# One encoder layer on one core: S5's transfers on another queue, weights asked for earlier, and smaller edits around them

## The chip, the core and the metric

The kernel runs on one core of a Trainium2 chip. The core has five engines with a queue of instructions each: TensorE (PE, matrix products into PSUM), VectorE (DVE), ScalarE (ACT), GpSimd (POOL) and SyncE (SP, which here issues DMAs only). DMAs can be issued from SP, ACT or POOL. An engine takes its instructions in the order of its queue; an instruction whose inputs aren't there holds up all behind it. The metric is the device time of one execution in microseconds (us); the profile's span runs from the first to the last instruction.

## What is computed

One layer of an encoder on 512 tokens of width 1024, all in float32. Cut to what matters:

```python
h = rms_norm(x, attn_norm_g)
a_q, a_ckv, a_iq, a_ik, a_iw, s5_u, c_qkv, c_z, c_a, c_b, gates = split(h @ w_in)
y_a = dsa_attention(a_q, a_ckv, a_iq, a_ik, a_iw, ...) @ w_proj_a   # top-128 keys of an indexer, then softmax
y_b = s5_branch(s5_u, ...) @ w_proj_b                               # complex diagonal recurrence, gelu, gated unit
y_c = gdn_branch(c_qkv, c_z, c_a, c_b, ...) @ w_proj_c              # gated delta rule in chunks of 64
g_a, g_b, g_c = split(sigmoid(gates))
x = x + (g_a * y_a + g_b * y_b + g_c * y_c) @ w_out
x = x + conv_glu_ffn(rms_norm(x, ffn_norm_g), w_up, ffn_conv_w, w_down)
return rms_norm(x, final_norm_g)
```

In `s5_branch` the last step is the gated unit, `y * sigmoid(y @ w_glu)`. In `gdn_branch` a triangular system of 64 rows is solved for each chunk and head; the kernel forms the inverse instead.

## The kernel before

**Products.** float32 accuracy comes from three fast products for each: `split` writes an operand as a high part (`wh`, an ACT cast) and a low part (`wl`, a DVE subtraction), and `dense` sums high x high, high x low and low x high. `wload` (L272) fetches a 128x1024 weight tile `w` by DMA from SP's queue and splits it; there are two buffers of `w` and two pairs `wh`, `wl` in the first half of the kernel. A third pair, `self.wx`, is foreseen but stays `None`. `proj(i)` (L326) loads tile i of `w_in` and runs the 24 matmuls of 128x512 into one of two PSUM buffers `ps_acc`; its caller empties the buffer. With GP = 3, behind the S5 stage every third load's low part is computed on POOL (L285) instead of DVE (L256).

**Stages up to the feed-forward part.** (1) Start: x and the first four weight tiles arrive, the tiles of `s5_u` are projected, the norm is formed (`rB`), `u` is stored to DRAM (`ud`, L1405) and the normed input is split into `hh`, `hl`. (2) S5: `s5_uu` (L570) reads U back from `ud`, for each half of the groups twice, into the lower and the upper 64 partitions; `s5_setup` and `s5_half` form tables; `s5_state` runs two scans a call, `s5_out` forms y and stores it to `yd` (L708); `s5_main` reads it back as `yT` (L602), splits it, multiplies by `w_glu`, and for each of four tiles computes tanh on ACT (L623), `(tanh + 1) * yT` on DVE (L624) and a permuted copy times 0.25 on ACT (`s_bo`, L628), which goes to DRAM (`obd`). Woven into it are the projections for 18 gates (`gates`, whose tanh is stored to DRAM from SP's queue, L1260) and rounds of the indexer's top-k (`topk`: MAX8 and MATCH_REPLACE on DVE). (3) The delta rule: 12 projections with a convolution on DVE (`gdn_in`, L753 to L758), then `gdn_main`, with attention's projections, the rest of the gates and the top-k woven in; `gdn_main` inverts the chunks' triangles: 16-row blocks on DVE (L902 to L927), then 32-row and 64-row blocks by small products on PE (L940 to L977), which are woven with attention and with `merge` of branch b. (4) The merges, `w_out`, the feed-forward part and the last norm.

**Order.** The Python code weaves these parts by hand (the strings `ORD`, `OR1`, `OR2`, `OR3` and the rates `R_...` say which generator gives the next step). The order of the code isn't yet that of the queues: the kernel is built with `schedule_with_timeline_sim=True`, and a planner simulates the engines by its own model of durations and fills each queue with what it holds ready, earlier code first. `issue_after` binds an instruction behind another on its engine. On the chip the queues run as planned, whatever the true durations are.

Of the kernel before, what the change touches and what calls it, by code (L numbers as in the profile page):

```python
# [157 lines left out]
GP = 3  # L158
KV = 'acc'
OR3 = 'ttgztgzttggtttttggzggttt'  # L160
XO = 'w0,t0,w0,t1,w1,t2,t3,x0,x1,x2,x3,w2'
# [12 lines left out]
NBIG = 5  # L174
R_QKV = 0.606
# [49 lines left out]
class _K:  # L225
# [46 lines left out]
    def wload(self, src, n=1024, hl=None):  # L272
# [4 lines left out]
        if hl is None:  # L277
            if self.wx and self.wi % 3 == 0:
                hl = [self.wx.tile([128, 1024], F32R, tag="x" + z, name="w" + z, bufs=1) for z in "hl"]
            else:  # L280
                hl = [self.wp.tile([128, 1024], F32R, tag="w" + z, name="w" + z, bufs=self.wb) for z in "hl"]
# [43 lines left out]

    def proj(self, i):  # L326
        wh, wl = self.wload(self.I["w_in"][i])
        ps = self.acc()
        self.dense(ps, wh, wl, self.hh, self.hl, 8)
        return ps  # L330
# [39 lines left out]
    def s5_setup(self):  # L370
# [27 lines left out]
        tt(t0, dt, P("are"), OP.mult)  # L398
        with self.tc.issue_after(self.lastp.ins):
            exact_exp(mag, t0)  # L400
# [168 lines left out]
    def s5_uu(self):  # L569
# [3 lines left out]
        v = self.ud.rearrange("(h b m) (j c) -> h (m j) b c", h=2, m=16, j=4)  # L573
        for hf in range(2):
            U = self.s5.tile([128, 16, 128], F32, tag="U", name="s5_U", bufs=2)
            for r in range(2):
                nc.sync.dma_start(U[r * 64:r * 64 + 64], v[hf])
# [3 lines left out]
    def s5_main(self):  # L581
        nc = self.nc
        self.yd = self.dp.tile([512, 512], F32, tag="yd", name="s5_yd", bufs=1)
        self.yyh, self.yyl = [], []
        self.s5q = []
# [14 lines left out]
        for n in range(4):  # L600
            t = self.s5.tile([128, 512], F32, tag="b2", name="s5_yT", bufs=self.nb2)
            nc.sync.dma_start(t, self.yd[n * 128:(n + 1) * 128])  # L602
# [9 lines left out]
        for n2 in range(2):  # L612
            wh, wl = glu[n2]
            for j in range(2):
# [9 lines left out]
                nc.vector.scalar_tensor_tensor(s, s, 1.0, yT[n], OP.add, OP.mult)  # L624
                sv = s.rearrange("p (t c) -> p t c", t=4)
                pv = lambda x: x.rearrange("p (c t) -> p t c", t=4)
                bo = self.s5.tile([128, 512], F32, tag="b2", name="s5_bo", bufs=self.nb2)
                nc.scalar.activation(pv(bo), sv, AF.Identity, scale=0.25)  # L628
                nc.sync.dma_start(obd[:, n], bo)
# [3 lines left out]
    def s5_state(self, hf, o, WT, CA, T, cosT, sinT, m4):  # L633
# [33 lines left out]
        sr = q.tile([128, 4, 129], F32, tag="sr", name="s5_sr", bufs=2)  # L667
        si = q.tile([128, 4, 129], F32, tag="si", name="s5_si", bufs=2)
        nc.gpsimd.memset(sr[:, :, 0:1], 0.0)
        nc.gpsimd.memset(si[:, :, 0:1], 0.0)  # L670
# [10 lines left out]
    def s5_out(self, hf, o, WT, CA, T, S):  # L681
# [17 lines left out]
        for g in range(2):  # L699
# [7 lines left out]
            for a2 in range(2):  # L707
                nc.sync.dma_start(yv[hf][g][a2], yy[rows[a2]].rearrange("p (b c) -> p b c", b=4))  # L708
# [66 lines left out]
    def gdn_main(self):  # L775
# [167 lines left out]
        for h0 in (0, 2):  # L943
# [8 lines left out]
            for h in range(2):  # L952
                pc = ps[:, h * 256:h * 256 + 256].rearrange("p (t a b) -> p t a b", b=32, t=4)
                tt(half(P1[h], 0).rearrange("p (t a) b -> p t a b", t=4), pc, _bc(half(self.C("m32"), 0), 1, 4), OP.mult)
            for h in range(2):
                pxy = self.acc("sm")
                for t in range(4):
                    c = slice(t * 128, (t + 1) * 128)
                    self.mm(pxy[0:64, 256 + t * 32:256 + t * 32 + 32], YF[0:64, h0 + h, t * 128:t * 128 + 64],
                            P1[h][0:64, t * 128:t * 128 + 32])  # L960
                    self.mm(pxy[:, t * 64:t * 64 + 64], P1[h][:, c], half(YF[:, h0 + h, c], 1))
# [5 lines left out]
        for h in range(4):  # L967
            ps = self.acc("sm")
            N4, X4, Y4, P4 = v4(NT[:, h]), v4(XF[:, h]), v4(YF[:, h]), v4(P1h())
            for t in range(4):  # L970
                self.mm(ps[64:128, t * 64:t * 64 + 64], N4[0:64, t, 64:128], X4[0:64, t, 0:64])
            nc.scalar.copy(P4[64:128, :, 0:64], ps[64:128, 0:256].rearrange("p (t c) -> p t c", t=4))
            py = self.acc("sm")
            for t in range(4):
                self.mm(py[0:64, t * 64:t * 64 + 64], P4[64:128, t, 0:64], Y4[64:128, t, 64:128])
            nc.scalar.copy(Y4[0:64, :, 64:128], py[0:64, 0:256].rearrange("p (t c) -> p t c", t=4))
            yield 1  # L977
# [146 lines left out]
    def attn(self):  # L1124
# [14 lines left out]

        def keys(j):  # L1140
# [6 lines left out]
            kl = [ap.tile([128, 512], F32R, tag="kl%d" % z, name="a_kl", bufs=2) for z in range(2)]  # L1147
# [470 lines left out]
```

## Time and profile before

| | us |
|---|---|
| median of 3 runs (lowest to highest) | 956.65 (956.61 to 957.61) |
| the profiled execution, its own time | 957.42 |
| its span | 955.7 |
| PE busy | 918.5 (96%) |
| DVE busy | 645.3 (68%) |
| ACT busy | 419.5 (44%) |
| POOL busy | 84.4 (9%) |

The profile is one execution. "Busy" of PE means that a matmul is under way; matmuls overlap, so what PE could do faster doesn't show in that number. A full matmul of 128x512 starts every 0.23 us at the clock of 2.4 GHz and every 0.43 us at 1.2 GHz; which of the two is granted stands in the column of the clock. The rows on which the prediction rests stand below, under the diff.

### The profile page before, as it was taken

To read this page: it belongs to the slowest core of one execution; us is meant where nothing else is said; L and a number is where in the kernel's file an instruction comes from. 1 tells how busy PE (TensorE), PEld (TensorE's weight loads), DVE (VectorE), ACT (ScalarE), POOL (GpSimd) and SP (SyncE) were. 2 spreads that over 40 slices of the span, in tenths; PEclk is the share of its full clock that TensorE was granted. 3 is DMA by queue.
4 is the path that set the end of the run, shared out by engine and by line. 5 is a ranking of instruction groups with operands and counts; after the bars stand their busy time and mean duration, and the time that the engine had idled before them with its cause. 6 is when DMAs were issued, how large, how long until landed. Compare 5 with 4: busy or idle time off the path is not lost. (4 is left out here: it accounts for less than half of the span.)

```text
span 955.7 us, 12705 instructions
## 1 busy us (share of the span) xinstructions
PE 918.5 (96%) x4780; PEld 746.2 (78%) x4780; DVE 645.3 (68%) x1119; ACT 419.5 (44%) x761; POOL 84.4 (9%) x93
## 2 busy tenths in 40 slices
PE   7989999896999999899999999999999999999997
PEld 5768877675888777778868888988888888888885
DVE  5969497988998779546677736667666676622423
ACT  6574443235565653237852314443444434322212
POOL 3001000110123411311011000000000000000000
PEclk9999999997999999989999999999999999999999
DMA  8585334441224645523108723232323223223212
GB/s 319 152 192 147 108 99 132 144 134 65 88 89 121 171 122 165 155 89 121 34 12 278 229 100 109 94 107 90 109 89 102 96 88 110 89 95 104 88 67 88
DMA packets 55917, 114.54 MB, mean 120 GB/s; under 512 B 15664, under 2 KB 22192, under 8 KB 55856
## 3 DMA queue, kind: packets, MB, share of 16 engines
q1 hardware_dynamic: 53776, 110.33, 36.4%
q0 software_dynamic: 2080, 3.41, 1.8%
q8 instruction: 37, 0.61, 0.3%
q14 instruction: 24, 0.20, 0.1%
HBM read 95.89 MB, written 14.42 MB: 115 GB/s over the span
## 5 line engine op out<-in xcount | busy, mean ns | idle before, releaser
L256 DVE TENSOR_TENSOR wl<-w,wh 128x1024 fp32r<-128x1024 f32 (+1 forms) x127 | 153.0, 1206 | 146.2 <-ACT wh L255 145.8
L255 ACT CAST wh<-w 128x1024 fp32r<-128x1024 f32 (+1 forms) x127 | 131.7, 1037 | 192.3 <-PE ps_acc L247 80.7
L247 PE MATMUL ps_acc<-hh,wh 128*128 128x512 f32 x376 | 152.6, 406 | 12.7 <-ACT g_raw L753 10.1
L247 PE MATMUL ps_acc<-hh,wl 128*128 128x512 f32 x376 | 151.6, 403 | 1.3 <-DVE wl L256 1.3
L247 PE MATMUL ps_acc<-hl,wh 128*128 128x512 f32 x376 | 149.5, 398 | 0.0
L247 PEld LDWEIGHTS ps_acc<-hh,wh 128*128 128x128 f32 x376 | 72.1, 192 | 28.7 <-ACT g_raw L753 10.5
L247 PEld LDWEIGHTS ps_acc<-hh,wl 128*128 128x128 f32 x376 | 72.0, 192 | 19.3 <-DVE wl L256 2.6
L247 PEld LDWEIGHTS ps_acc<-hl,wh 128*128 128x128 f32 x376 | 72.1, 192 | 15.4 <-issue 0.5
L247 PE MATMUL ps_acc<-f_hh,wh 128*128 128x512 f32 x160 | 62.3, 389 | 0.0
L247 PE MATMUL ps_acc<-f_hl,wh 128*128 128x512 f32 x160 | 62.3, 389 | 0.0
L247 PE MATMUL ps_acc<-f_hh,wl 128*128 128x512 f32 x160 | 62.2, 389 | 0.0
L247 PE MATMUL ps_sm<-f_hh,wh 128*128 128x512 f32 x160 | 62.2, 389 | 0.0
L247 PE MATMUL ps_sm<-f_hl,wh 128*128 128x512 f32 x160 | 62.2, 389 | 0.0
L247 PE MATMUL ps_sm<-f_hh,wl 128*128 128x512 f32 x160 | 62.2, 389 | 0.0
L285 POOL TENSOR_TENSOR wl<-w,wh 128x1024 fp32r<-128x1024 f32 x13 | 34.9, 2687 | 186.2 <-ACT wh L284 171.1
L255 ACT CAST ah<-f_th 128x512 fp32r<-128x512 f32 x22 | 13.7, 621 | 58.1 <-DVE f_th L1554 58.1
L247 PEld LDWEIGHTS ps_acc<-f_hl,wh 128*128 128x128 f32 x160 | 30.0, 188 | 6.3
L247 PEld LDWEIGHTS ps_sm<-f_hh,wh 128*128 128x128 f32 x160 | 30.1, 188 | 6.2
L247 PEld LDWEIGHTS ps_acc<-f_hh,wl 128*128 128x128 f32 x160 | 30.1, 188 | 6.2
L247 PEld LDWEIGHTS ps_sm<-f_hl,wh 128*128 128x128 f32 x160 | 30.0, 188 | 6.2
L247 PEld LDWEIGHTS ps_sm<-f_hh,wl 128*128 128x128 f32 x160 | 30.0, 187 | 6.2
L247 PEld LDWEIGHTS ps_acc<-f_hh,wh 128*128 128x128 f32 x160 | 30.0, 187 | 6.1
(532 smaller groups left out, 1984.4 us busy)
## 6 DMA issues: line engine op xcount, KB each, us to landing
w<-in_w_in_dram SPq DMA_DIRECT2D x50, 512.0 KB, 3.6
w<-in_w_up_dram SPq DMA_DIRECT2D x44, 512.0 KB, 3.3
w<-in_w_down_dram SPq DMA_DIRECT2D x22, 512.0 KB, 3.3
gd<-m_th SPq DMA_DIRECT2D x24, 256.0 KB, 2.2
m_th<-gd SPq DMA_DIRECT2D x24, 256.0 KB, 3.7
w<-in_w_out_dram SPq DMA_DIRECT2D x8, 512.0 KB, 4.3
sq<-in_x_dram SPq DMA_DIRECT2D x4, 512.0 KB, 8.9
s_U<-s_ud SPq DMA_DIRECT2D x4, 512.0 KB, 8.9
```

What stands on the lines that cost most here:

```text
L247: return self.nc.tensor.matmul(out, lhsT, rhs, start=start, stop=stop)
L255: self.lasta = nc.scalar.copy(hi, src)
L256: self.lastv = nc.vector.tensor_sub(lo, src, hi.bitcast(F32))
L285: nc.gpsimd.tensor_tensor(l[:, :n], w[:, :n], h[:, :n].bitcast(F32), OP.subtract)
```

## The change

- S5's transfers go to POOL's queue: the store of `u` of the start, the reads of U, the store and the read back of `yd`, the store of `obd`. U is read in quarters into the lower 64 partitions, and the upper 64 are copied from the lower ones within SBUF.
- The gated unit: DVE writes the permuted `bo` itself; ACT's copy is gone, and the factor 0.25 is applied in `fetch`, by the split.
- Inverse products: in the 32-row step all products of one shape come first and then those of the other, for two heads at once; in the 64-row step two heads share a PSUM tile and a copy.
- Weights: `proj` takes its pair from a list that `ahead` fills: after the matmuls of a projection, the loads of the next two (in S5 three) are put into the code, in the order `PLAN`. In S5 the pair `wx` exists, for every third load of the first 20.
- GP = 0: no weight split on POOL.
- Stores of gates go from ACT's queue. The states' tiles `sr`, `si` are four fixed ones, whose first column is cleared once. The zero halves of the keys `kl` are written for the first two of four only.
- At the start: `rB` is cleared and 12 products of 128x128 on it run first; w2 is asked for before the rows of x; `t0` and `mag` of S5's setup wait for the split of the fourth weight tile.

```diff
@@ -155,10 +155,10 @@
...
-GP = 3
+GP = 0
...
-XO = 'w0,t0,w0,t1,w1,t2,t3,x0,x1,x2,x3,w2'
+XO = 'w0,t0,w0,t1,w1,t2,t3,w2,x0,x1,x2,x3'
@@ -172,6 +172,9 @@
...
+PLAN = [27, 28, 29, 30, 31, 21, 22, 32, 33, 34, 35, 36, 37, 38, 39, 40, 41, 42, 43, 44, 8, 9, 10, 11, 4, 5, 6, 7, 12, 13, 14, 15,
+        20, 16, 17, 18, 19, 45, 46, 23, 47, 24, 48, 49, 50, 25, 26]
+N_WX = 20
@@ -269,13 +272,13 @@
...
-    def wload(self, src, n=1024, hl=None):
+    def wload(self, src, n=1024, hl=None, extra=False):
...
-            if self.wx and self.wi % 3 == 0:
+            if self.wx and extra and self.fpos % 3 == 0:
@@ -323,10 +326,23 @@
...
+    def ahead(self, n):
...
+        while len(self.fq) < n and self.fpos < len(PLAN):
+            i = PLAN[self.fpos]
+            self.fpos += 1
+            keep = self.lasta, self.lastv
+            w = self.wload(self.I["w_in"][i], extra=self.fpos <= N_WX)
+            self.fq.append((i, w, self.lasta, self.lastv))
+            self.lasta, self.lastv = keep
...
-        wh, wl = self.wload(self.I["w_in"][i])
+        self.ahead(1)
+        j, (wh, wl), self.lasta, self.lastv = self.fq.pop(0)
+        assert i == j
...
+        self.ahead(3 if self.fpos < N_WX else 2)
@@ -395,8 +411,9 @@
...
-        tt(t0, dt, P("are"), OP.mult)
-        with self.tc.issue_after(self.lastp.ins):
+        with self.tc.issue_after(self.lastw.ins):
+            tt(t0, dt, P("are"), OP.mult)
+        with self.tc.issue_after(self.lastp.ins), self.tc.issue_after(self.lastw.ins):
@@ -570,11 +587,12 @@
...
-        v = self.ud.rearrange("(h b m) (j c) -> h (m j) b c", h=2, m=16, j=4)
+        v = self.ud.rearrange("(n b m) (j c) -> n (m j) b c", n=4, m=16, j=4)
...
-            for r in range(2):
-                nc.sync.dma_start(U[r * 64:r * 64 + 64], v[hf])
+            for z in range(2):
+                nc.gpsimd.dma_start(U[0:64, z * 8:z * 8 + 8], v[hf * 2 + z])
+            nc.gpsimd.dma_start(U[64:128], U[0:64])
@@ -582,6 +600,12 @@
...
+        self.sri = []
+        for z in range(2):
+            x = [self.s5.tile([128, 4, 129], F32, tag="s%s%d" % (c, z), name="s5_s" + c, bufs=1) for c in "ri"]
+            for y in x:
+                nc.gpsimd.memset(y[:, :, 0:1], 0.0)
+            self.sri.append(x)
@@ -599,7 +623,7 @@
...
-            nc.sync.dma_start(t, self.yd[n * 128:(n + 1) * 128])
+            nc.gpsimd.dma_start(t, self.yd[n * 128:(n + 1) * 128])
@@ -621,12 +645,11 @@
...
-                nc.vector.scalar_tensor_tensor(s, s, 1.0, yT[n], OP.add, OP.mult)
-                sv = s.rearrange("p (t c) -> p t c", t=4)
-                pv = lambda x: x.rearrange("p (c t) -> p t c", t=4)
...
-                nc.scalar.activation(pv(bo), sv, AF.Identity, scale=0.25)
-                nc.sync.dma_start(obd[:, n], bo)
+                tc_ = lambda x: x.rearrange("p (t c) -> p t c", t=4)
+                nc.vector.scalar_tensor_tensor(bo.rearrange("p (c t) -> p t c", t=4), tc_(s), 1.0, tc_(yT[n]), OP.add, OP.mult)
+                nc.gpsimd.dma_start(obd[:, n], bo)
@@ -664,10 +687,7 @@
...
-        sr = q.tile([128, 4, 129], F32, tag="sr", name="s5_sr", bufs=2)
-        si = q.tile([128, 4, 129], F32, tag="si", name="s5_si", bufs=2)
-        nc.gpsimd.memset(sr[:, :, 0:1], 0.0)
-        nc.gpsimd.memset(si[:, :, 0:1], 0.0)
+        sr, si = self.sri[o // 4]
@@ -705,7 +725,7 @@
...
-                nc.sync.dma_start(yv[hf][g][a2], yy[rows[a2]].rearrange("p (b c) -> p b c", b=4))
+                nc.gpsimd.dma_start(yv[hf][g][a2], yy[rows[a2]].rearrange("p (b c) -> p b c", b=4))
@@ -952,29 +972,43 @@
...
+            pxys = [self.acc("sm") for h in range(2)]
...
-                pxy = self.acc("sm")
...
-                    self.mm(pxy[0:64, 256 + t * 32:256 + t * 32 + 32], YF[0:64, h0 + h, t * 128:t * 128 + 64],
+                    self.mm(pxys[h][:, t * 64:t * 64 + 64], P1[h][:, c], half(YF[:, h0 + h, c], 1))
+            for h in range(2):
+                for t in range(4):
+                    self.mm(pxys[h][0:64, 256 + t * 32:256 + t * 32 + 32], YF[0:64, h0 + h, t * 128:t * 128 + 64],
...
-                    self.mm(pxy[:, t * 64:t * 64 + 64], P1[h][:, c], half(YF[:, h0 + h, c], 1))
+            for h in range(2):
+                pxy = pxys[h]
...
-        for h in range(4):
-            ps = self.acc("sm")
-            N4, X4, Y4, P4 = v4(NT[:, h]), v4(XF[:, h]), v4(YF[:, h]), v4(P1h())
-            for t in range(4):
-                self.mm(ps[64:128, t * 64:t * 64 + 64], N4[0:64, t, 64:128], X4[0:64, t, 0:64])
-            nc.scalar.copy(P4[64:128, :, 0:64], ps[64:128, 0:256].rearrange("p (t c) -> p t c", t=4))
+        ht4 = lambda x, h: x[:, h:h + 2].rearrange("p h (t d) -> p (h t) d", t=4)
+        x64 = lambda x: x.rearrange("p (x c) -> p x c", c=64)
+        P4s = []
+        for h in (0, 2):
+            ps, P4 = self.acc("sm"), P1h()
+            N4, X4 = ht4(NT, h), ht4(XF, h)
+            for x in range(8):
+                self.mm(ps[64:128, x * 64:x * 64 + 64], N4[0:64, x, 64:128], X4[0:64, x, 0:64])
+            nc.scalar.copy(P4[64:128], ps[64:128])
+            P4s.append(P4)
+        yield 1
+        yield 1
+        for h, P4 in zip((0, 2), P4s):
...
-            for t in range(4):
-                self.mm(py[0:64, t * 64:t * 64 + 64], P4[64:128, t, 0:64], Y4[64:128, t, 64:128])
-            nc.scalar.copy(Y4[0:64, :, 64:128], py[0:64, 0:256].rearrange("p (t c) -> p t c", t=4))
-            yield 1
+            Y4 = ht4(YF, h)
+            for x in range(8):
+                self.mm(py[0:64, x * 64:x * 64 + 64], P4[64:128, x * 64:x * 64 + 64], Y4[64:128, x, 64:128])
+            nc.scalar.copy(Y4[0:64, :, 64:128], x64(py[0:64]))
+        yield 1
+        yield 1
@@ -1137,6 +1171,8 @@
...
+        kls = [[rt("kl%d%d" % (i, z), 1)[:, 0] for z in range(2)] for i in range(2)]
@@ -1144,10 +1180,11 @@
...
-            kl = [ap.tile([128, 512], F32R, tag="kl%d" % z, name="a_kl", bufs=2) for z in range(2)]
+            kl = kls[j % 2]
...
-                nc.gpsimd.tensor_scalar(kl[z][o], self.C("ones")[o, 0:1].broadcast_to([64, 512]), 0.0, None, OP.mult)
+                if j < 2:
+                    nc.gpsimd.tensor_scalar(kl[z][o], self.C("ones")[o, 0:1].broadcast_to([64, 512]), 0.0, None, OP.mult)
@@ -1247,7 +1284,7 @@
...
-            self.split(h[:, j], l[:, j], t)
+            self.split(h[:, j], l[:, j], t, 0.25)
@@ -1257,7 +1294,7 @@
...
-            nc.sync.dma_start(gd, th)
+            nc.scalar.dma_start(gd, th)
@@ -1303,6 +1340,7 @@
...
+        self.fq, self.fpos = [], 0
@@ -1343,6 +1381,11 @@
...
+                nc.gpsimd.memset(self.rB, 0.0)
+                pw = self.acc("po")
+                for i in range(12):
+                    self.mm(pw[:, :128], self.rB[:, :128], self.rB[:, 128:256])
@@ -1390,6 +1433,7 @@
...
+                self.lastw = self.lastv
@@ -1402,7 +1446,7 @@
...
-                    sync(self.ud[n * 128:(n + 1) * 128], uv)
+                    nc.gpsimd.dma_start(self.ud[n * 128:(n + 1) * 128], uv)
@@ -1427,12 +1471,14 @@
...
+                self.wx = s.enter_context(self.pool("wx", bufs=1))
...
+                self.wx = None
```

## Rows read from the trace of the kernel before

**Rows 1.** The page, its first part: busy time of TensorE (PE), share of the span, instructions.
```profile
PE 918.5 (96%) x4780; PEld 746.2 (78%) x4780; DVE 645.3 (68%) x1119; ACT 419.5 (44%) x761; POOL 84.4 (9%) x93
```

**Rows 2.** The list of waits of PE over the whole execution: the operation that waited, what it waited for, us in total, times, the longest.
```profile
PE ps_acc L247 <- ACT g_raw L753: 10.1, 1, 10.1
...
PE ps_acc L247 <- ACT wh L255: 2.6, 1, 2.6
PE ps_acc L247 <- DVE g_k L768: 2.5, 1, 2.5
```

**Rows 3.** The busy time of each engine by stretch. Columns: the stretch in us from the span's start, its length, then us busy and (in brackets) instructions of PE, PE's weight loads, DVE, ACT and POOL, then the granted clock of PE (1.00 is 2.4 GHz, and half of it 1.2 GHz), the busy share of the DMA engines, GB/s.
```profile
24.00:48.00 24.00, 23.27 (x104) 17.60 (x103) 23.75 (x54) 13.02 (x24) 1.51 (x4) 1.00 0.51 154
...
72.00:96.00 24.00, 24.00 (x172) 19.66 (x170) 22.00 (x37) 11.51 (x20) 4.08 (x8) 1.00 0.55 151
...
58.00:68.00 10.00, 6.85 (x22) 5.14 (x22) 6.27 (x16) 6.58 (x11) 0.00 (x0) 0.83 0.64 216
176.00:198.00 22.00, 18.48 (x147) 14.14 (x146) 19.11 (x25) 6.24 (x9) 4.10 (x1) 0.92 0.47 145
205.00:232.00 27.00, 16.34 (x59) 12.39 (x58) 24.42 (x67) 13.88 (x21) 1.68 (x3) 0.75 0.21 76
382.00:392.00 10.00, 7.49 (x30) 5.63 (x29) 6.87 (x9) 1.54 (x2) 6.46 (x7) 0.83 0.41 76
408.00:422.00 14.00, 14.00 (x65) 11.33 (x63) 5.73 (x21) 4.38 (x13) 0.00 (x0) 0.76 0.23 82
...
168.00:312.00 144.00, 129.82 (x677) 104.45 (x674) 131.43 (x256) 71.42 (x164) 23.67 (x18) 0.94 0.35 108
```

**Rows 4.** The timeline of PE in 224 to 231. Columns: start in us, length in us, engine, line, operation, tiles written <- read, shapes, count, and in square brackets the idle time just before and what ended it. A length reaches into the next matmul; the pace is the difference of two starts.
```profile
224.18 0.80 PE L247 MATMUL ps_acc<-hh,wh 128*128 128x512 f32 x1 [10.11 <-ACT g_raw L753]
...
229.80 0.40 PE L247 MATMUL ps_acc<-hl,wh 128*128 128x512 f32 x1
230.03 0.40 PE L247 MATMUL ps_acc<-hh,wl 128*128 128x512 f32 x1
```

**Rows 5.** The timelines of ACT at the end of the gated unit (first three rows) and of DVE (the last operation of the unit, and L1404, an operation with permuted operands at 32).
```profile
222.09 1.11 ACT L628 ACTIVATE s_bo<-s_gl 128x512 f32<-128x512 f32 x1 [1.68 <-DVE s_gl L624]
223.00 0.65 ACT L751 ACTIVATE g_k<-ps_acc,cw 128x512 f32<-128x512 f32 x1
223.54 0.58 ACT L753 COPY g_raw<-ps_acc 128x512 f32<-128x512 f32 x1
...
32.01 1.04 DVE L1404 TENSOR_TENSOR sq<-ps_pt,rB 128x512 f32<-128x512 f32 x1
...
221.38 0.67 DVE L624 SCALAR_TENSOR_TENSOR s_gl<-s_gl,s_yT 128x512 f32<-128x512 f32 x1
```

**Rows 6.** The weight splits (`wl`) of the whole execution on DVE and on POOL, from the fifth part of the page (count, us busy, mean ns of one, idle before); then the timelines of POOL and DVE at 182 and of DVE at 382.
```profile
L256 DVE TENSOR_TENSOR wl<-w,wh 128x1024 fp32r<-128x1024 f32 (+1 forms) x127 | 153.0, 1206 | 146.2 <-ACT wh L255 145.8
...
L285 POOL TENSOR_TENSOR wl<-w,wh 128x1024 fp32r<-128x1024 f32 x13 | 34.9, 2687 | 186.2 <-ACT wh L284 171.1
...
182.02 4.10 POOL L285 TENSOR_TENSOR wl<-w,wh 128x1024 fp32r<-128x1024 f32 x1 [7.82 <-ACT wh L284]
...
182.71 1.21 DVE L665 TENSOR_TENSOR_SCAN s_rb<-s_m4t,s_ra 128x512 f32<-128x512 f32 x1
183.84 3.36 DVE L666 TENSOR_TENSOR_SCAN s_rd<-s_m4t,s_rc 128x512 f32<-128x512 f32 x1
...
382.93 2.34 DVE L925 COPY g_Xa<-g_W 64x128 f32<-64x128 f32 x1
385.30 0.27 DVE L926 COPY g_Ya<-g_W 64x128 f32<-64x128 f32 x1
```

**Rows 7.** DMA issues in 43 to 62 (tiles, queue, count, KB each, median us from issue to landing) and, in the same columns, `a_qh` over the whole execution; the timeline of POOL's queue at 82; then of the tile view of `s_U` the products of the states (shortest, median and longest ns, first and last start), and of the tile view of `s_yd` the issue and the landing.
```profile
s_U<-s_ud SPq DMA_DIRECT2D x4, 512.0 KB, 8.9
w<-in_w_in_dram SPq DMA_DIRECT2D x3, 512.0 KB, 8.8
...
a_qh<-sp_h POOLq DMA_DIRECT2D x4, 128.0 KB, 4.3
...
82.34 1.02 POOL L269 DMA_DIRECT2D a_iq<-sp_h  x2 [35.34 <-ACT sp_h L266]
...
L247 PE MATMUL ps_pt<-s_U,s_wt x128: 269/269/321, 95.6 to 169.0; 64*64 64x128 f32 x128
...
L708 SPq DMA_DIRECT2D s_yd<-s_yy x8: 575/606/627, 163.9 to 200.1; - x8
...
DMA to landing us min/median/max: 2.4/3.0/3.6
```

**Rows 8.** The timeline of PE in the inverse: runs of one shape (at 391 and 422), and two starts of the alternating pairs (at 398 and 399).
```profile
391.14 1.97 PE L247 MATMUL ps_sm<-g_X,g_NT 128*128 128x64 f32 x16
...
398.56 0.30 PE L247 MATMUL ps_sm<-g_P,g_Y 64*64 64x32 f32 x2
...
399.16 0.30 PE L247 MATMUL ps_sm<-g_P,g_Y 64*64 64x32 f32 x2
...
422.25 0.68 PE L247 MATMUL ps_sm<-g_X,g_NT 64*64 64x64 f32 x8
```

**Rows 9.** The timeline of PE near the start.
```profile
11.44 0.63 PE L247 MATMUL ps_acc<-xh,wl 128*128 128x512 f32 x1
...
14.43 0.49 PE L247 MATMUL ps_acc<-xh,wl 128*128 128x512 f32 x1
```

## The prediction, made before the change was built

> **What bounds the kernel now.** I read the page first: TensorE (PE) is busy for 96% of the span [rows 1]. So the question is what PE loses and where. Three views tell that, in this order: PE's list of waits, the sums of busy time by stretch, and the timelines of single engines around each loss.
>
> The waits [rows 2]: 10.1 us in one piece for the copy `g_raw`, 2.6 us for a weight `wh`, 2.5 us for `g_k`. The stretches [rows 3] show idle time (length less PE busy) and the granted clock together. PE idles 3.15 us in 58 to 68, 3.5 us in 176 to 198, 10.7 us in 205 to 232 and 2.5 us in 382 to 392, and behind each of these the clock falls to 1.2 GHz for some us. Where PE works on, a clock share below one is time lost too: (1 - 0.83) x 10 = 1.7 us in the first, 0.08 x 22 = 1.8 us in the second, 1.7 us in the fourth, and 0.24 x 14 = 3.4 us in 408 to 422, where PE never idles. In the third, PE resumes at 224.18 and needs 5.6 us for 13 matmuls, against 13 x 0.23 = 3.0 us at 2.4 GHz [rows 4]: 2.6 us. Together this is 31 us, all of it before 422; the wait at the very start, 6 us for the first inputs, and the feed-forward part behind 530 are not touched. VectorE (DVE) is the second engine: it works 131.4 of 144 us in 168 to 312 and 23.75 of 24 us in 24 to 48 [rows 3].
>
> **The change part by part.** Sums are against the profiled execution, 957.42 us (span 955.7 and 1.7 us around it), which is 0.8 us above the median of the three runs, 956.65.
>
> *A. The gated unit (206 to 230).* PE stands from 214.07 to 224.18 because both `ps_acc` buffers are full. ScalarE (ACT) empties them at 223.00 and 223.54, but in its queue the four copies `s_bo` come first, and each waits for DVE's `s_gl` (the last one 1.7 us for the `s_gl` of 221.38), which stands in DVE's queue among the rounds of the top-k [rows 5]. The change removes these copies: DVE writes `bo` in its place, and the factor 0.25 goes into the split of `fetch` (the same number of instructions, with a scale; 0 to +0.4 us, beside PE's work). ACT then waits for PE alone: after the last product a tanh (some 0.6, as L753 on the same shape), L751 (0.65) and L753 (0.58 us), so 1.9 us of wait instead of 10.1: 8.2 us, and with the clock's 2.6 us 10.8. The new DVE write is permuted; the permuted L1404 takes 1.04 us against 0.67 for L624 [rows 5], so 4 x 0.37 = 1.5 us of DVE.
>
> *B. No weight split on GpSimd (GP = 0).* 13 splits of 2.69 us leave POOL, and DVE gets 13 x 1.21 = 15.7 us [rows 6]. But POOL's splits cost DVE already: the scan at 183.84 takes 3.36 us beside one, the scan just before it 1.21 us; the copy at 382.93 takes 2.34 us, its like at 385.30 0.27 us [rows 6]. That is 2.1 us in each of these; if all 13 cost so much, DVE gains 12 us in sum, if the other 11 cost nothing, it loses 11. I count its load as unchanged. The scan's 2.15 us is what PE waits for at 190 (1.5 us, clock 1.8 us): 3.3 us of possible gain. In 382 to 392 PE waits for `g_k` behind the slow copy: 2.07 us come off, 1.21 us come on if the split falls in the same place, so 0.9 to 2.1 us of 2.5, and the clock if the rest is short (1.7). I take 2.
>
> *A and B together* have a cap: in 168 to 312 DVE has 131.4 us of work, and 1.5 us more. PE's losses there are 14 us, but the stretch can't be shorter than 133: with DVE full, as in 24 to 48, it gives 11 us, with DVE at today's 91% nothing. I take 8, nearer to the full stretch, since the rounds of the top-k that fill DVE now wait for nobody until attention and can move later.
>
> *C. Weights ahead, third pair, S5 transfers (58 to 68).* The weight that PE waits for at 60.7 was asked for while four transfers of U, 512 KB each in 512-byte runs, were under way: they take 8.9 us to land, and the weights beside them 8.8 us [rows 7]. Now U is read from DRAM once and its other half copied inside SBUF in long rows, so there are half as many short runs; with the third pair a cast can also start a projection (24 x 0.23 = 5.5 us) earlier. 4.8 us can go; I take 4. Behind S5 there are two pairs as before: asking earlier can't give more than the buffers, and I count it at 0. The gate stores now stand in ACT's queue, behind their own tanh. The trace has no transfer issued by ACT; the nearest row is POOL's 0.51 us [rows 7], 24 of them 12 us of an engine that is busy 13.9 of 27 us in 205 to 232 [rows 3]. Queued behind each are the next cast and the next evacuation of a `ps_acc`; the 5.5 us of a projection cover them. 0, between -1 (SP no longer holds weights back behind a store) and +2.
>
> *POOL's queue itself.* ud, U, yd, yT and bo leave SP's queue for POOL's, past which now go the key copies, `a_iq` and the memsets. POOL issues 64-row transfers at 0.51 us each [rows 7]; the trace has none with 256 (yd) or 512 runs (U), so 0.5 us each, or by runs 2.0 and 4.1 us. U is wanted only at 95.6 [rows 7], and even 4 x 4.1 us and four landings of 8.9 us, one after another from 43 on, are over at 95. The last yd and yT lie on a path: their issue is 0.61 us each on SP and their landing 3.0 us; on POOL 0.5 to 2.0 us, twice for yd and once for yT, and landings up to 4.3 us like `a_qh` [rows 7]: 0 to +6 us (3 x 1.4 and 2 x 1.3, rounded down by the shorter yT). I take 0, as POOL's 0.51 us is the nearest row.
> The Trainium skill (DMA: Bandwidth & Descriptors, section "SWDGE vs HWDGE vs iDMA") speaks against this part: POOL writes its descriptors into rings in SBUF, from which DVE locks it out in some of its modes, while transfers issued from SP are "immune to that interference". Here DVE is busy 22.0 of 24 us in 72 to 96 [rows 3] and POOL's issue still takes 0.51 us, so nothing of that shows at 64 rows; by the rule the +6 us end would hold, whose consequences are the rival "POOL's queue" below.
>
> *D. Grouped inverse products (398 to 442).* Today 16 pairs alternate between a 64-row and a 128-row shape, 0.60 us a pair. Runs of one shape cost 1.97/16 = 0.12 and 0.68/8 = 0.085 us an instruction [rows 8], two of each to a pair: 0.42 us. 16 x 0.18 = 2.9 us, on a PE that never idles in 408 to 422 [rows 3]. The 3.4 us of low clock in the same stretch follow these sparse products; whether they go I can't say from a row: 0 to 3.4, I take 2. The rest of the inverse does the same products with half the copies. Sum 5.
>
> *E. The start.* The 12 products on zeros let PE reach 2.4 GHz before its first real ones; 7 matmuls that now take 3.0 us [rows 9] would take 1.6. But then DVE, full in 24 to 48, sets the pace: 0, between -1.4 and +0.6 (if the dummies last beyond the arrival of the first inputs). That `mag` now waits for the fourth weight, and w2 is asked for before x: 0, up to +2, as DVE's small steps fit anywhere.
>
> *New waits.* The planner lays out all queues anew. It left PE 20 us of idle time in the four places above; how many such places it makes this time no row says. I add 1 us, up to +6, since most of these had a cause that is removed.
>
> Sum: -8 -2 -4 -5 +1 = -18: 957.4 - 18 = 939.4, and 0.8 less on the scale of the median: **938.6 us**.
>
> **The rivals.**
> *Everything is collected:* A and B 11, then 4.2, 4.8, 6.3 and 1.4 us: 27.7 us, 928.9. For it: the losses have separate causes. Against it: DVE at 100%.
> *DVE takes PE's place as the bound:* in 168 to 312 nothing is gained, as DVE stays at its 91%; then -2 -4 -5 +1 = -10: 946.6. For it: 131.4 of 144 us.
> *No gain:* the new queues stall PE elsewhere as much as today, 20 us, against gains of 19: 956.6. For it: the stall of 10 us was the planner's own order. Against it: it takes as many mishaps as now.
> *POOL's queue, the slower side.* If POOL's issue goes by runs (8 ns each), the last yd and yT come 6 us late. ACT's queue then stands at the casts of `s_yhl`, and the evacuations of `ps_acc` stand behind these, so A's 8 and B's 2 are not collected, 6 us and a fall of the clock (2.6 us) are added, and U's landings push `a_iq` (wanted from 82 on) by 5 us: -4 -5 +1 +6 +2.6 +5 = +5.6: 962.2. It decides from some 1.5 us per 256-run transfer; against it stand POOL's transfers of today, landed in 4.3 us.
>
> **How the numbers follow.** Forecast 0.50 (932 to 944), all collected 0.14, DVE 0.18, no gain 0.08, POOL's queue 0.10. The range takes in the first three and part of the fourth: **927 to 952**. A measurement here can tell about 0.2% from no change. Faster by more: the first three and a little of the fourth, 0.83; within 0.2%: most of the fourth, 0.06; slower: the fifth and a rest of the fourth, 0.11.
>
> **What would show it.** A right: no `s_bo` on ACT, PE's longest wait under 3 us. B: no DVE scan above 1.3 us, no wait for `g_k` above 1.5. C: the first casts of S5 don't wait for a DMA. D: 64-row products in runs, PEclk at full from 408 to 422. DVE's rival: DVE above 95% from 168 to 300 and PE's waits named after DVE. POOL's rival: DMA_DIRECT2D of yd on POOL above 1.5 us, ACT waiting for `s_yT`. The forecast is wrong if PE shows a new wait above 5 us before 422, or if the time behind 422 changes by more than 2 us.

## The result, and the profile after

| | before | after |
|---|---|---|
| median, us (lowest to highest, 4 runs each) | 956.84 (956.61 to 957.61) | 942.59 (942.41 to 943.95) |
| the profiled execution, own time / span, us | 957.42 / 955.7 | 942.50 / 940.7 |

The ratio is 0.9851 (95% interval 0.9816 to 0.9886): 14.2 us faster, where 18 were forecast, within the range of 927 to 952.

The page of after, first part, then PE's waits over the whole execution (us in total, times, the longest):

```profile
PE 910.5 (97%) x4804; PEld 744.1 (79%) x4804; DVE 642.9 (68%) x1132; ACT 415.3 (44%) x753; POOL 59.5 (6%) x99
```

```profile
PE ps_acc L250 <- ACT m_th L1296: 2.8, 2, 1.9
PE ps_sm L250 <- DMA g_X<-g_xd: 2.8, 1, 2.8
PE ps_acc L250 <- ACT g_raw L773: 2.5, 2, 1.7
...
PE ps_acc L250 <- DVE g_k L788: 1.5, 1, 1.5
```

The 10.1 us for `g_raw` [rows 2] are 2.5 now; a wait of 2.8 us for `g_X` is new. Where the time went is seen best in sums over long stretches (the columns of rows 3), first of before, then of after:

```profile
0.00:168.00 168.00, 157.77 (x945) 122.33 (x947) 128.45 (x262) 89.75 (x139) 14.48 (x35) 0.99 0.54 164
...
168.00:232.00 64.00, 49.82 (x296) 38.95 (x293) 57.77 (x115) 25.17 (x38) 7.70 (x5) 0.87 0.37 119
...
360.00:400.00 40.00, 37.05 (x166) 29.51 (x164) 31.22 (x40) 12.11 (x19) 11.96 (x10) 0.96 0.53 154
400.00:505.00 105.00, 102.67 (x721) 82.68 (x721) 65.98 (x182) 63.38 (x173) 14.20 (x7) 0.97 0.24 77
```

```profile
0.00:168.00 168.00, 157.12 (x1022) 123.31 (x1023) 137.73 (x277) 89.24 (x138) 23.23 (x47) 0.99 0.52 162
...
168.00:232.00 64.00, 59.90 (x295) 47.77 (x293) 55.73 (x117) 25.91 (x40) 8.06 (x14) 1.00 0.41 132
...
360.00:400.00 40.00, 35.71 (x183) 29.99 (x182) 23.84 (x45) 10.91 (x19) 7.44 (x8) 0.91 0.52 149
400.00:505.00 105.00, 102.04 (x718) 82.73 (x718) 69.65 (x179) 61.62 (x163) 2.94 (x1) 1.00 0.33 108
```

Up to 168 us nothing is gained: PE is busy for 157.1 us against 157.8, at the same clock, although its weights come earlier. The stall at 60.7 that part C was priced by is gone (58 to 68 in after; 6.85 us busy at 0.83 in [rows 3]):

```profile
58.00:68.00 10.00, 10.00 (x45) 8.22 (x45) 5.92 (x21) 8.57 (x13) 0.00 (x0) 1.00 0.90 256
```

But others stand around it: 2.8 us for `m_th`, the tanh of a gate on ACT, in two pieces that end at 57.8 and 75.4, and 2.4 us in 40 to 47 for `wl`, `hl` and `ik` of DVE. Nearly all is earned in 168 to 232, 10.1 us less idle time and the full clock. In 360 to 400 some is lost again (4.3 us idle against 2.95, clock 0.91 against 0.96), and in 400 to 505 the clock is full now (0.97 before). The inverse's first products start at 378.77, 12.4 us earlier than before [rows 8]; the spans differ by 15.0. So 12.4 us come from ahead of the inverse, 2.6 from the inverse on.

The gated unit in after, on ACT and then on PE (columns as in rows 5 and 4):

```profile
208.46 0.60 ACT L647 ACTIVATE s_gl<-ps_pt 128x512 f32<-128x512 f32 x1 [1.34 <-DVE s_bo L651]
...
212.09 0.60 ACT L647 ACTIVATE s_gl<-ps_pt 128x512 f32<-128x512 f32 x1 [1.99 <-PE ps_pt L250]
212.58 0.68 ACT L771 ACTIVATE g_k<-ps_acc,cw 128x512 f32<-128x512 f32 x1
213.15 0.59 ACT L773 COPY g_raw<-ps_acc 128x512 f32<-128x512 f32 x1
```

```profile
213.79 0.50 PE L250 MATMUL ps_acc<-hh,wh 128*128 128x512 f32 x1 [1.74 <-ACT g_raw L773]
```

After the last product a tanh, L771, L773, then PE: 1.74 us, as forecast (1.9). But the third tanh waits 1.34 us for DVE's `s_bo`: the tiles `s_gl`, `s_bo` and `yT` share one tag of seven buffers (`b2`), and a buffer has to come free. Here PE still has products to do, so the wait is covered.

The inverse in after, timeline of all engines (`w_kv` is a weight of attention):

```profile
371.16 0.33 SPq L1169 DMA_DIRECT2D w<-in_w_kv_dram  x1
...
371.65 0.45 SPq L952 DMA_DIRECT2D g_xd<-g_Xa  x1
...
372.99 0.50 PE L250 MATMUL ps_acc<-f_h,wh 128*128 128x512 f32 x1 [1.54 <-DVE g_k L788]
...
375.21 1.92 SPq L959 DMA_DIRECT2D g_X<-g_xd  x4
...
378.77 3.65 PE L250 MATMUL ps_sm<-g_X,g_NT 128*128 128x64 f32 x16 [2.75 <-DMA g_X<-g_xd]
```

The same on SP's queue in before:

```profile
385.30 0.45 SPq L932 DMA_DIRECT2D g_xd<-g_Xa  x1
...
387.58 1.92 SPq L939 DMA_DIRECT2D g_X<-g_xd  x4
...
391.72 0.43 SPq L1135 DMA_DIRECT2D w<-in_w_kv_dram  x1
```

The 16-row blocks go to DRAM and back, from the first store's issue to the first product, in 7.1 us in after and in 5.8 us in before (385.30 to 391.14 [rows 8]), where PE didn't wait. Two things differ. In after the 512 KB load of `w_kv` is issued just ahead of the stores, in before behind the reads; the reads follow 3.56 us behind the first store, against 2.28. And in front of the inverse PE has 12 products, which `g_k` releases 1.3 us behind that store in both; they take 3.0 us in after (372.99 to 376.02, full clock) and 4.5 us in before (386.63 to 391.14, most of them at 1.2 GHz). 1.3 and 1.5 us make the 2.75. The first holds in every trace here: the reads follow 3.4 to 3.8 us behind the store in the ten where the load stands just ahead of it, and 2.3 us in the four where it doesn't.

### The profile page after: what moved, and what is told of

It reads as the page before. It is cut to its first block, busy times and chain, and to the rows that moved or that the text cites. A ratio compares the mean times of both kernels' runs of the same rounds, so it can differ in the third digit from the quotient of the medians.

```text
span 940.7 us, 12731 instructions
## 1 busy us (share of the span) xinstructions
PE 910.5 (97%) x4804; PEld 744.1 (79%) x4804; DVE 642.9 (68%) x1132; ACT 415.3 (44%) x753; POOL 59.5 (6%) x99
## 4 chain that ended last, share of the span: by engine, by line
PE 77%; DVE 12%; issue 3%; ACT 3%; DMA 3%; SPq 0%; POOL 0%; ACTq 0%; POOLq 0%; DVEq 0%
PE ps_acc L250 40%; PE ps_sm L250 20%; PE ps_pt L250 11%; PE ps_po L250 4%; DVE a_wk L1111 1%; DVE wl L259 1%; PE ps_pt L253 1%; DVE a_m L1110 1%; PE ps_sm L253 1%; DMA w<-in_w_in_dram 1%; ACT wh L258 1%; DMA xt<-in_xt_dram 1%; DVE ht L1465 1%; DVE s_rb L688 0%; DMA s_yT<-s_yd 0%
## 5 line engine op out<-in xcount | busy, mean ns | idle before, releaser
L259 DVE TENSOR_TENSOR wl<-w,wh 128x1024 fp32r<-128x1024 f32 (+1 forms) x140 | 168.8, 1207 | 142.9 <-ACT wh L258 142.8
L258 ACT CAST wh<-w 128x1024 fp32r<-128x1024 f32 (+1 forms) x140 | 145.4, 1039 | 220.8 <-PE ps_acc L250 120.1
L250 PE MATMUL ps_acc<-hh,wl 128*128 128x512 f32 x376 | 148.6, 396 | 0.9 <-DVE wl L259 0.9
L1598 ACT ACTIVATE f_th<-f_a 128x512 f32<-128x512 f32 x22 | 13.9, 633 | 45.2 <-DVE f_a L1595 45.2
```

The costliest lines, as they stand in the source:

```text
L250: return self.nc.tensor.matmul(out, lhsT, rhs, start=start, stop=stop)
L258: self.lasta = nc.scalar.copy(hi, src)
L259: self.lastv = nc.vector.tensor_sub(lo, src, hi.bitcast(F32))
L1598: nc.scalar.activation(th, tl[0], AF.Tanh)
```

## The experiments

**Theory**, from the prediction: each part takes away its own loss (A with B 8 us, C 4 around 58 to 68, D 5). **Rivals:** DVE becomes the bound in 168 to 312; or the parts are not separate, and one pays only beside another. The runs of one kernel spread by 2 to 12 us here, so ratios to the kernel before stand with their intervals. The yardstick is the changed kernel itself (`a_again`), run on the chip of `b_bogp`, `u_ahead` and `u_grp`; the others ran on two more chips, and the kernel before took 957.7, 957.7 and 958.2 us on the three:

> The changed kernel itself, on the same chip as the three beside it, as their yardstick: 0.985 of the kernel before, some 942 to 944 us.

Measured: 942.81 us (941.39 to 944.39), 0.9844 (0.9821 to 0.9866).

### Parts A and B alone, on the kernel before

`b_bo` (A), `b_gp` (B) and `b_bogp` (both):

```diff
-                nc.vector.scalar_tensor_tensor(s, s, 1.0, yT[n], OP.add, OP.mult)
...
-                nc.scalar.activation(pv(bo), sv, AF.Identity, scale=0.25)
+                nc.vector.scalar_tensor_tensor(bo.rearrange("p (c t) -> p t c", t=4), tc_(s), 1.0, tc_(yT[n]), OP.add, OP.mult)
...
-            self.split(h[:, j], l[:, j], t)
+            self.split(h[:, j], l[:, j], t, 0.25)
```

```diff
-GP = 3
+GP = 0
```

> The kernel before with part A alone (no s_bo copy on ACT in the gated unit, DVE writes bo, factor 0.25 in fetch's split). By parts: PE's wait of 10.1 us for g_raw falls to about 2 us and the slow clock behind it goes, so 8 to 11 us faster than before, 946 to 949 us. Rival, DVE takes PE's place as the bound: the wait comes back under other names between 168 and 312 us, less than 2 us gained, 955 to 957 us.

> The kernel before with part B alone (GP = 0, all weight splits on DVE). By parts: the 3.36 us scan at 184 and the 2.34 us copy at 383 become short, 2 to 5 us faster, 952 to 955 us; the wait of 10 us for g_raw stays. Rival: 13 splits of 1.21 us more on a DVE that is busy 91% between 168 and 312 us, so PE's waits for DVE grow there and the time is the same or up to 5 us longer, 956 to 962 us.

> The kernel before with parts A and B together (no s_bo copy on ACT, no splits on POOL), no weights asked for ahead, nothing on POOL's queue, inverse products as before. Alone, A gave 0.18% and B cost 0.38%. If the two need each other, since either alone leaves a stall in the same stretch of DVE's queue, they give together the 8 us of the prediction, 946 to 950 us. If A pays only where weights are asked for ahead, they give 3 us or less together, 954 to 960 us, with PE's waits in 190 to 312 us named after wl or g_raw.

Measured: A alone 0.9982 (0.9958 to 1.0006), 956.2 us; B alone 1.0038 (1.0013 to 1.0063), 961.5 us; both 0.9951 (0.9931 to 0.9971), 953.0 us. A alone gave next to nothing (the interval takes in 1), B alone cost 3.6 us, together 4.7 us are gained. The traces of A and of B are of the slowest of their ten executions (961.98 and 965.5 us). A's timeline, ACT and PE:

```profile
215.74 0.60 ACT L623 ACTIVATE s_gl<-ps_pt 128x512 f32<-128x512 f32 x1 [1.74 <-DVE s_bo L627]
...
217.45 0.79 PE L247 MATMUL ps_acc<-hh,wh 128*128 128x512 f32 x1 [3.32 <-ACT g_raw L752]
```

The wait of 10.1 us is 3.3, not 1.9: two tanhs stand for `s_bo` (1.87 and 1.74 us), the last until 215.74. Of the 6.7 us that PE resumes earlier, 1.9 are left at the inverse (389.21 against 391.14); part was given back in waits named after DVE (240 to 312):

```profile
PE ps_acc L247 <- DVE wl L256: 1.5, 1, 1.5
PE ps_acc L247 <- DVE sp_l L267: 1.1, 1, 1.1
```

In 240 to 312 DVE is busy 67.9 of 72 us, and PE idles 2.8 us there, where it didn't before. For A alone the rival is right. B alone leaves the 10 us where they were and adds waits elsewhere, by its list of waits:

```profile
PE ps_acc L247 <- ACT g_raw L753: 10.0, 1, 10.0
...
PE ps_pt L247 <- ACT s_yhl L255: 3.5, 1, 3.5
PE ps_sm L247 <- DMA g_X<-g_xd: 3.0, 1, 3.0
```

In this trace the inverse starts 0.8 us later than in before, and 7.1 of the 7.9 us that the span is longer lie behind its start, where the clock in 400 to 505 is 0.92 (0.97 in before). The wait for `g_X` is there without any part but B, and with PE no earlier: the load of `w_kv` (384.18) has moved ahead of the store (384.68), as in after.

### Is DVE the bound after the change?

`t_half`: every second round of the top-k left out.

```diff
         for rd in range(16):
-            for qt in (3, 2, 1):
+            for qt in (3, 2, 1) if rd % 2 == 0 else ():
```

> The kernel after with every second round of the indexer's top-k left out (8 of 16; the masks then keep 64 keys instead of 128; nothing else changes). It takes some 25 us of DVE work out of the stretch from 190 to 290 us. If DVE, busy 100% of 192 to 216 and of 240 to 288, sets the pace there after the change, the time falls by 3 us or more, to below 940. If PE sets the pace and the rounds only fill DVE, the time moves by less than 1.5 us, 941 to 944.

Measured: 939.39 us, 0.9812 (0.9788 to 0.9837), 3.4 us under the yardstick, with intervals that overlap. By the time alone that looks like DVE; the stretches say otherwise (columns of rows 3):

```profile
168.00:232.00 64.00, 60.34 (x290) 48.15 (x290) 44.40 (x82) 27.26 (x42) 8.10 (x14) 0.97 0.41 137
232.00:360.00 128.00, 128.00 (x611) 104.12 (x610) 102.94 (x182) 72.84 (x187) 13.64 (x22) 1.00 0.43 123
360.00:400.00 40.00, 37.34 (x210) 31.17 (x208) 25.63 (x53) 12.36 (x25) 7.43 (x7) 0.96 0.52 151
```

With 11 us less DVE work in 168 to 232, PE is busy 60.3 us there against 59.9, and it works through 232 to 360 in both; over 190 to 290, DVE's work falls from 98.4 to 78.6 us, and PE is busy 98.0 us against 97.5. The gain is in 360 to 400, where PE idles 2.7 us in place of 4.3 and the clock is 0.96 in place of 0.91: DVE comes to the 16-row blocks of the inverse sooner (their first store is issued at 369.16, against 371.65 in after and 370.26 in `a_again`). So DVE doesn't set PE's pace where A, B and C earn; the little that is gained, if it is more than noise, comes at the start of the inverse.

### Part A undone in the changed kernel

`u_bo`: ACT's copy is back (the first diff reversed, the store still on POOL's queue).

> The kernel after with part A undone (ACT's permuted copy times 0.25 is back; its DMA stays on POOL's queue). By parts: PE's long wait for g_raw comes back, 8 to 11 us, 950 to 954 us. Rival: the new order (weights ahead, no splits on POOL) already keeps PE fed in 205 to 232, so undoing A costs less than 3 us, below 946.

Measured: 950.23 us, 0.9927 (0.9900 to 0.9955): 7.4 us slower than the yardstick. The wait for `g_raw` is back, in one piece of 7.0 us. So A is worth much more here than on the kernel before (1.5 us, with an interval that takes in no change).

### Weights ahead, and the third pair

`u_ahead` (neither) and `u_wx` (weights two ahead everywhere, no third pair):

```diff
-        self.ahead(3 if self.fpos < N_WX else 2)
...
-                self.wx = s.enter_context(self.pool("wx", bufs=1))
```

```diff
-        self.ahead(3 if self.fpos < N_WX else 2)
+        self.ahead(2)
...
-                self.wx = s.enter_context(self.pool("wx", bufs=1))
```

> The kernel after with the weights asked for as before (proj loads its own pair, no list, no third pair); everything else of the change stays. By the prediction, part C is worth 4 us and only before 70 us: 945 to 948 us. If asking ahead is what lets part A pay, the waits in 190 to 240 us return too and it costs 8 us or more, above 950 us.

> The kernel after without the third pair of buffers, but with weights still asked for ahead, two projections everywhere. Asking ahead was worth 9 us (951.9 against 942.8). If that comes from the order it gives behind 150 us, where there are two pairs in any case, little is lost: 943 to 945 us. If it comes from the third pair in S5, most of it is lost: 949 to 952 us.

Measured: 951.88 us, 0.9943 (0.9925 to 0.9961), and 953.3 us, 0.9950 (0.9932 to 0.9968). Without the third pair some 10 us are lost, whether weights are asked for ahead or not. The loss is not where C was placed. The stretches of `u_wx`, then of after:

```profile
96.00:120.00 24.00, 24.00 (x184) 19.87 (x183) 11.52 (x18) 10.93 (x16) 0.00 (x0) 1.00 0.31 107
...
192.00:240.00 48.00, 38.20 (x185) 29.87 (x179) 40.84 (x96) 19.61 (x31) 8.06 (x14) 0.93 0.29 99
```

```profile
96.00:120.00 24.00, 23.57 (x203) 19.01 (x202) 20.56 (x34) 13.00 (x19) 0.10 (x1) 1.00 0.20 67
...
192.00:240.00 48.00, 45.45 (x202) 36.82 (x201) 47.17 (x110) 21.99 (x35) 4.43 (x8) 1.00 0.31 105
```

PE loses 7.25 us of idle time and 0.07 x 48 = 3.4 us of clock in 192 to 240, together 10.6, as much as is lost. Where it begins lies 100 us earlier: in 96 to 120 PE is full in both, but DVE works 11.5 us in one and 20.6 in the other. What DVE waits for there, by line, in 96 to 132, `u_wx` and then after (count, us busy, mean ns, idle before):

```profile
L259 DVE TENSOR_TENSOR wl<-w,wh 128x1024 fp32r<-128x1024 f32 x4 | 4.9, 1226 | 8.3 <-ACT wh L258 8.2
```

```profile
L259 DVE TENSOR_TENSOR wl<-w,wh 128x1024 fp32r<-128x1024 f32 x4 | 4.9, 1223 | 1.5 <-ACT wh L258 1.5
```

And what ACT's casts wait for there, first `u_wx`, then after:

```profile
L258 ACT CAST wh<-w 128x1024 fp32r<-128x1024 f32 x4 | 4.2, 1048 | 3.0 <-PE ps_acc L250 2.6 <-ACT m_th L1296 0.5
```

```profile
L258 ACT CAST wh<-w 128x1024 fp32r<-128x1024 f32 x5 | 5.3, 1052 | 1.0 <-PE ps_acc L250 1.0
```

With two pairs the next weight can't be cast until PE has finished a projection; DVE stands 8.3 us at the split that follows the cast, and S5's steps stand behind it in DVE's queue. So S5's scans come 15 to 17 us earlier with the third pair (views of L688: shortest, median and longest ns, first and last start). The waits of DVE in 96 to 132 make 8.9 us of that (6.7 at the split and 2.2 where DVE waits for the indexer's `a_rel` of ACT); the rest is how the planner ordered DVE's queue. After and then `u_wx`:

```profile
L688 DVE TENSOR_TENSOR_SCAN s_rb<-s_m4t,s_ra x4: 1203/1212/1215, 110.2 to 170.4; 128x512 f32<-128x512 f32 x4
```

```profile
L688 DVE TENSOR_TENSOR_SCAN s_rb<-s_m4t,s_ra x4: 1205/1216/1219, 127.4 to 185.7; 128x512 f32<-128x512 f32 x4
```

Projections are left over, and PE does them while S5's last transfers and the gated unit run. Without the third pair they are used up by then (PE in `u_wx`):

```profile
203.93 6.74 PE L250 MATMUL ps_pt<-s_yhl,s_glw 128*128 128x512 f32 x21 [3.27 <-ACT s_yhl L258]
...
221.52 0.57 PE L250 MATMUL ps_acc<-hh,wh 128*128 128x512 f32 x1 [3.17 <-ACT g_raw L773]
```

`u_ahead` shows the same two waits, 3.1 us for `s_yhl` and 6.8 us in two pieces for `g_raw`.

### Grouping undone

`u_grp`: the 32-row and 64-row steps as before.

```diff
-                    self.mm(pxys[h][:, t * 64:t * 64 + 64], P1[h][:, c], half(YF[:, h0 + h, c], 1))
...
+                    self.mm(pxy[0:64, 256 + t * 32:256 + t * 32 + 32], YF[0:64, h0 + h, t * 128:t * 128 + 64],
+                            P1[h][0:64, t * 128:t * 128 + 32])
+                    self.mm(pxy[:, t * 64:t * 64 + 64], P1[h][:, c], half(YF[:, h0 + h, c], 1))
```

> The kernel after with part D undone (the inverse products again pair by pair, one head at a time). By the prediction D is worth 2.9 us of products and 2 us of clock: 946 to 949 us. Rival: PE waits for the inverse's DMA and runs at the slow clock around it either way, so grouping gives less than 2 us, 942 to 945 us.

Measured: 950.22 us (945.82 to 952.19, 5 runs), 0.9915 (0.9887 to 0.9943): 7.4 us by the medians. The profiled execution is the fastest of the five; its span is 944.0, 3.3 us over after's. PE in `u_grp`, then in after:

```profile
388.87 0.30 PE L250 MATMUL ps_sm<-g_P,g_Y 64*64 64x32 f32 x2
...
389.46 0.30 PE L250 MATMUL ps_sm<-g_P,g_Y 64*64 64x32 f32 x2
```

```profile
391.13 0.55 PE L250 MATMUL ps_sm<-g_Y,g_P 128*128 128x64 f32 x4
391.61 0.65 PE L250 MATMUL ps_sm<-g_P,g_Y 64*64 64x32 f32 x8
```

A pair takes 0.59 us alternating; grouped, four of one shape take 0.48 us and eight of the other 0.65, so 2 x 0.12 + 2 x 0.08 = 0.40. 16 x 0.19 = 3.0 us is most of the span's difference. The other four runs of `u_grp` have mean clocks of 0.983 to 0.989 against 0.993 in the profiled one, and are 2.6 to 6.4 us longer: that is D's clock term, which comes and goes without the grouping. In which stretch those runs lost it no trace of `u_grp` shows, but the other traces point to 400 to 505: the clock there is 1.00 in all nine with the grouping, and 0.92 (`b_gp`), 0.95 (`b_bo`), 0.97 (before), 1.00 (`b_bogp`) and 1.00 (`u_grp`) in the five without. 0.08 of 105 us is 8.4 us.

### S5's transfers back on SP's queue

`u_sp` (the same in five places):

```diff
-                nc.gpsimd.dma_start(U[0:64, z * 8:z * 8 + 8], v[hf * 2 + z])
+                nc.sync.dma_start(U[0:64, z * 8:z * 8 + 8], v[hf * 2 + z])
```

> The kernel after with S5's transfers back on SP's queue (ud, the quarters of U and their copy in SBUF, yd, yT, bo); the rest stays. By the prediction the queue is worth nothing: 942 to 945 us. If SP's queue holds weights back behind these transfers' waits, as loads are now asked for ahead, it costs 3 us or more: above 945. If POOL's slower issue (0.62 us against 0.61 for yd, but 0.57 for yT) and the chain yd to yT cost what the rival said, undoing it gains: below 941.

Measured: 941.62 us, 0.9820 (0.9796 to 0.9845): the interval overlaps the yardstick's, no difference. The issue of two `yd` stores and (last line of each) store to landing, in `u_sp` and in after:

```profile
184.80 1.25 SPq L728 DMA_DIRECT2D s_yd<-s_yy  x2
```

```profile
s_yd<-s_yy SPq DMA_DIRECT2D x4, 128.0 KB, 2.5
```

```profile
183.38 1.23 POOL L728 DMA_DIRECT2D s_yd<-s_yy  x2 [21.44 <-DVE s_yy L726]
```

```profile
s_yd<-s_yy POOLq DMA_DIRECT2D x4, 128.0 KB, 3.6
```

Both queues need 0.62 us a store; from POOL it lands 1.1 us later, which PE's projections cover.

### The start as before

`u_start`:

```diff
-XO = 'w0,t0,w0,t1,w1,t2,t3,w2,x0,x1,x2,x3'
+XO = 'w0,t0,w0,t1,w1,t2,t3,x0,x1,x2,x3,w2'
...
-                for i in range(12):
-                    self.mm(pw[:, :128], self.rB[:, :128], self.rB[:, 128:256])
```

(and `t0`, `mag` unbound).

> The kernel after with the start as before (no products on zeros, w2 asked for last, t0 and mag of S5's setup not bound behind the fourth weight). By the prediction worth 0, between -0.6 and +1.4: 942 to 944.5 us. The trace of after is 1.3 us ahead at the last product of the start, so 944 is what that lead would give if it lasts.

Measured: 941.22 us, 0.9822 (0.9798 to 0.9847): no difference that the intervals allow. PE's wait for the first inputs is 7.4 us there, against 1.7, but that lead doesn't last: in 12 to 48 PE idles 0.95 us in `u_start` and 3.36 us in after.

### The inverse's reads from two queues

`i_xs`, an attempt to better the changed kernel:

```diff
-                nc.sync.dma_start(g16(F)[s, :, s], xd[z][b].rearrange("g i k -> i g k"))
+                (nc.sync, nc.scalar)[b % 2].dma_start(g16(F)[s, :, s], xd[z][b].rearrange("g i k -> i g k"))
```

> The kernel after, but the eight reads of the inverse's blocks (g_X, g_Y from xd) are issued in turn from SP and from ACT, so that the four of g_X are asked for within 1 us instead of 1.92. PE has the same order of products. If the wait of 2.75 us at 378.8 is this chain's, it gets about 1 us shorter, and more if the clock doesn't fall behind it: 938 to 942 us. If ACT stands at the two issues and comes late for its casts, no gain: 942.5 to 944 us.

Measured: 942.48 us, 0.9834 (0.9810 to 0.9859): no gain, and for neither expected reason. The timeline:

```profile
375.37 0.86 SPq L959 DMA_DIRECT2D g_X<-g_xd  x2
375.42 0.89 ACTq L959 DMA_DIRECT2D g_X<-g_xd  x2
...
378.85 1.44 PE L250 MATMUL ps_sm<-g_X,g_NT 128*128 128x64 f32 x8 [2.78 <-DMA g_X<-g_xd]
```

The issues end at 376.3 and not at 377.13, and PE starts at 378.85, as before. The reads land later by as much, in 2.7 us (SP) and 3.1 us (ACT) against 2.3. So it isn't the issue that bounds them; whether it is the transfers themselves, 64 KB each in rows of 128 bytes, or the four reads of `g_Y`, which now start 0.9 us earlier too (376.33 against 377.22), no run separates. The Trainium skill (DMA: Bandwidth & Descriptors, section "Issuing engines are not separate DMA queues") says that transfers of all issuing engines run on the same 16 DMA engines, so that a second issuer saves only the issue; here even that 0.8 us was not seen at PE.

## Why the prediction was right, and where not

The forecast was -18 us, of which -14.2 came. The sum holds by terms that were partly wrong: C brought some 5 us more than its price, A with B 3 less, and new waits more than 1 us. That these cancelled so well is luck.

- **A, mechanism.** Right: the copies behind DVE made the wait, and 1.74 us are left of it. Wrong: "ACT then waits for PE alone". The tanhs wait for DVE's `s_bo`, as the buffers are shared; alone, A leaves 3.3 us. A alone gained 1.5 us and not 8; it pays (7.4 us) in the changed kernel, beside the third pair.
- **B.** Right in its row: no scan above 1.22 us. The 2 us in 382 to 392 were not collected: the wait for `g_k` went from 2.5 to 1.5 us, and behind it PE now waits 2.75 us for `g_X`, as it does with B alone (3.0). B alone costs 3.6 us.
- **A and B together.** 8 forecast, 4.7 measured without C.
- **C.** The step that failed. It was priced at its own wait in 58 to 68, 4 us. That wait is gone, but others took its place (a cast still waits 1.25 us for its weight at 59), and at 168 there is no lead in PE's busy time. 9 to 10 us hang on C all the same, in 168 to 232 and through S5's place in DVE's queue; "I count it at 0" for all behind S5 was the error. "Asking earlier can't give more than the buffers" held: without the third pair, asking ahead gave nothing.
- The undone parts add up to more than the whole (7.4 + 10.5 + 7.4 us against 14.2): A and the third pair each bring back much the same loss. Put in one after the other on one chip (before, `b_bogp`, `u_ahead`, `a_again`: 957.7, 953.0, 951.9, 942.8 us), A with B brings 4.7 us, D with the queues and the start 1.1, and C 9.1.
- **D.** 5 forecast (2.9 of work, 2 of clock). The work is 3.0 to 3.3 us, the medians say 7.4; in 400 to 505 the clock is full. Right in the work. The clock term is a spread and not a size: the traces without the grouping lose between nothing and 8.4 us there.
- **POOL's queue, ACT's stores, the start: 0.** Right for the first and, within the noise, for the last. The gate stores were not tried by themselves, nor whether the new waits for `m_th` come from them. The Trainium skill's rule on POOL's rings (DMA: Bandwidth & Descriptors, section "SWDGE vs HWDGE vs iDMA") didn't decide: with DVE busy 16.5 of 24 us in 168 to 192, POOL's issue takes as long as SP's, and only the landing is 1.1 us longer; whether DVE was in one of those modes there, the trace doesn't say. The rival took 8 ns a run, 4.1 us for two stores; they take 1.23.
- **New waits, +1.** Too small: `g_X` 2.75 and the low clock around it, `m_th` 2.8, 1.65 us more idle time in 24 to 48 (21.62 us busy in after, against 23.27 in [rows 3]). In before the reads of `g_X` were issued from 387.58 on and PE came to their products at 391.14 [rows 8]; that the cover was so short was to be seen. It was long enough only as its products ran at 1.2 GHz: with A alone, whose chain is nearly as long as in before (6.0 us against 5.8), they ran at the full clock, and PE waits 1.6 us. (The rival "no gain" sums 20 against 19 to nothing; it would be 957.6 and not 956.6, which changes no chance.)
- **DVE's rival.** Right for A alone on the kernel before; wrong for the whole change, as `t_half` shows.

What stays open: how much of S5's earlier place is the buffer itself and how much the planner's new order, which can't be changed apart; `u_wx` takes away the third pair and the third load ahead together; and the third pair alone on the kernel before was not tried. What loses the clock in 400 to 505 in some executions and not in others no run shows.

## What to carry to other kernels

A stall is not always removed where it is read: if it ends a stretch in which the filler work ran out, find the queue that held the other work back, even 100 us earlier, and look there for a missing buffer. Price parts that feed the same stall together, and test each alone and each undone; the two differ by what the parts share. When a chain of transfers was just covered, count its cover anew after a change: the products in front of it get shorter at the full clock, and a load that moves ahead of it in the queue makes the chain longer.

## What the hardware showed that was not expected

Four reads of 64 KB in rows of 128 bytes landed no sooner when issued from two queues at once (2.7 and 3.1 us each, against 2.3 one after another). Where a load of 512 KB was issued 0.5 us ahead of a store of 128 KB, the reads that wait for the store were issued 3.4 to 3.8 us behind it, and 2.3 us where it wasn't. And a store of 256 rows took POOL 0.62 us to issue, as SP: the count of rows, which decided the slower rival, hardly shows in POOL's issue time (0.51 us for 64 rows, 0.62 for 256, 0.69 for the 512 of a quarter of U).
